# Down projections in blocks of seven products, their sums carried out by ScalarE and accumulating transfers

## The chip, the cores and the metric

The kernel runs on one NeuronCore of a Trainium2 chip. Its engines are TensorE (PE in the profile; PEld is its weight load), VectorE (DVE), ScalarE (ACT), GpSimd (POOL) and SyncE (SP); each works off its own instructions in order and waits on semaphores. Matmuls write into PSUM, which has eight banks of 128 x 512 float32. The metric is device time in microseconds, from the first to the last work of an execution; lower is better.

## The reference, cut to what matters

A two-layer model over 512 tokens with 1024 features. Each layer mixes tokens (spatial gating in the first, attention in the second, both with attention over 256 memory rows) and then has a feed forward with 2816 hidden features:

```python
f = rmsnorm(h, ln_ffn_pre[layer])
f = (jax.nn.silu(f @ w_ffn_gate[layer]) * (f @ w_ffn_up[layer])) @ w_ffn_down[layer]
h = h + rmsnorm(f, ln_ffn_post[layer])
```

All data are float32. The change concerns the last product, `@ w_ffn_down`: (512 x 2816) by (2816 x 1024).

## The kernel before, in words

**Three products for one.** A float32 operand is cut by `split` (L239) into a high part (ScalarE's cast to float32r) and a low part (VectorE's source minus high). `mm3` (L191 to L193) makes a product of three matmuls: high by high, high by low, low by high. So each weight block costs a cast on ScalarE and a subtraction on VectorE before TensorE can use it. Parts of weights stand in eight pairs of slots (tags `hi` and `lo`), raw weights as loaded from memory in four slots of 512 KB (tag `raw`); a split waits for a free pair of slots, a load for a free raw slot. All loads are issued by SyncE.

**The feed forward** (`feed_forward`, L1113) takes the 22 tiles of 128 hidden features in groups. Tiles 0 and 1 are computed at the boundary with the layer's mixing part and their down projection starts the sums `ys[tb][dh]` (four blocks of 128 tokens by two halves of 512 outputs, in SBUF). Then come the groups (2, 8), (8, 14), (14, 18) and (18, 22). For each pair of tiles in a group a `Seven` (L1018) computes gate, and another up: seven products in place of eight over two by two blocks (a Strassen scheme), each product four `mm3` of 256 columns. Its weight sums run on VectorE (`sums`, L1037), its results go to `s1` and `s2` (tag `p`, six slots of 128 x 512) partly by ScalarE's copies out of PSUM (L1059 to L1074) and partly by VectorE's additions (`end`, L1079 to L1082). `gate_rows` (L1132) multiplies by the norm and applies silu, `up_rows` (L1138) multiplies gate and up and splits the product into `fs`, the stationary operand of the down projection. In a `Seven` TensorE uses the PSUM banks of tag `mm` (gate) or `lg` (up), three each; two more have the tag `tr`.

**The down projection of a group** (L1191 to L1200) follows its Sevens: for each half `dh` of the outputs, four PSUM banks, one for each block of tokens; for each pair of hidden tiles a load (`down_weights`), two splits, and 2 x 4 `mm3` of 512 columns; at the end four additions on VectorE (L1200) of a bank onto `ys`. The last group, (18, 22), goes to `tail_of`, which completes the sums and the norm.

**Order.** The kernel is written as a program of tile operations; the framework orders each engine's instructions ahead of time by the order of the program and by a simulated readiness, and adds the semaphores. A tile that is allocated where all slots of its tag are taken waits for the release of one. `behind` adds an order by hand; here it keeps the weight sums of a group's first Seven behind the end of the Seven before.

Of the kernel before, what the change touches and what calls it, by code (L numbers as in the profile page):

```python
# [15 lines left out]
P = 128  # L16
# [3 lines left out]
TB = T // P  # L20
# [13 lines left out]
HALVES = ((0, 256), (256, 512))  # L34
# [6 lines left out]
def hybrid(ctx: ExitStack, tc: tile.TileContext, i: dict, out: bass.AP):  # L41
    nc = tc.nc
# [3 lines left out]
    tp = ctx.enter_context(tc.tile_pool(name="temps", bufs=4))  # L46
    wp = ctx.enter_context(tc.tile_pool(name="weights", bufs=4))
# [17 lines left out]
    def prob(s, shape=(P, T)):  # L65
        return tp.tile(list(shape), F32, tag="p", name=name(s), bufs=6)

    def temp(s, shape=(P, T), tag="t", bufs=4, dt=F32):
        return tp.tile(list(shape), dt, tag=tag, name=name(s), bufs=bufs)

    def small(s, n=4, dt=F32):
        return sp.tile([P, n], dt, tag=f"s{n}", name=name(s))

    def ps(tag, shape=(P, T), s="ps"):
        return pp.tile(list(shape), F32, tag=tag, name=name(s), bufs=2 if tag == "tr" else 3)

    V, A, PE, G = nc.vector, nc.scalar, nc.tensor, nc.gpsimd
# [53 lines left out]
    def pair_of_parts(n=512, aside=False):  # L131
        if aside:
            return act("whi"), act("wlo")
        return (wp.tile([P, max(n, 512)], F32R, tag="hi", name=name("whi"), bufs=8)[:, :n],
                wp.tile([P, max(n, 512)], F32R, tag="lo", name=name("wlo"), bufs=8)[:, :n])

    def cut(pair, w):

        return [(pair[0][:, d : d + w], pair[1][:, d : d + w]) for d in range(0, pair[0].shape[1], w)]
# [24 lines left out]
    def moving_pair(src, aside=False):  # L164

        raw = wp.tile([P, 1024], F32, tag="raw", name=name("raw"), bufs=4)
        last_load[0] = nc.sync.dma_start(raw.rearrange("p (m c) -> p m c", m=4), src)
        four = raw.rearrange("p (m k c) -> p m k c", m=4, k=2)
        parts = []
        for x in range(2):  # L170
            hi, lo = (t.rearrange("p (m c) -> p m c", m=4) for t in pair_of_parts(aside=aside))
            split(four[:, :, x, :], hi, lo)
            parts.append((hi, lo))
        return parts
# [5 lines left out]
    def down_weights(layer, k, dh, aside=False):  # L180
        return moving_pair(i["w_down"][layer, 4 * dh : 4 * dh + 4, :, k : k + 2, :]
                           .rearrange("m p k c -> p m (k c)"), aside)

    def token_products(o, x, w, tb, start, stop):

        c = slice(tb * P, (tb + 1) * P)
        return mm3(o.rearrange("p (m c) -> p m c", c=P), (x[0][:, c], x[1][:, c]), w, start, stop)

    def mm3(o, w, x, start, stop, more=False):

        PE.matmul(o, w[0], x[0], start=start, stop=False, skip_group_check=more)  # L191
        PE.matmul(o, w[0], x[1], start=False, stop=False, skip_group_check=more)  # L192
        return PE.matmul(o, w[1], x[0], start=False, stop=stop, skip_group_check=more)  # L193
# [44 lines left out]
    def split(src, hi, lo, eng=None):  # L238
        last_parts[:] = A.copy(hi, src), (eng or V).tensor_sub(lo, src, hi)  # L239
# [22 lines left out]
    class Norm:  # L262


        def __init__(self, width=T):
            self.r4 = small("r4")
            self.acc, self.width = None, width
# [66 lines left out]
    def parts(s):  # L334
        return [(act(f"{s}hi"), act(f"{s}lo")) for _ in range(KT)]
# [682 lines left out]
    class Seven:  # L1018
# [29 lines left out]
        def product(self, o, w, n, more=False):  # L1048
            for k, w in enumerate(cut(w, P)):
                mm3(o, w, self.xs[n][k], k == 0 and not more, k == KT // 2 - 1, more)  # L1050
# [62 lines left out]
    def feed_forward(layer, phase, xp, meanwhile=None):  # L1113

        nnorm = PairNorm()
        rb = rbc
        groups = ((2, 8), (8, 14), (14, 18), (18, 22))

        def hidden(gate, up, f, cols):
            c0, c1 = cols  # L1120
            n = c1 - c0
            gr = temp("gr")
            V.tensor_mul(gr[:, :n], gate, rb[:, c0:c1])
            s = temp("silu")
            A.activation(s[:, :n], gr[:, :n], AF.Silu)
            ff = temp("f")
            V.tensor_mul(ff[:, :n], up, s[:, :n])
            split(ff[:, :n], f[0][:, c0:c1], f[1][:, c0:c1])

        gates = [None] * 3  # L1130

        def gate_rows(row, g):  # L1132

            V.tensor_mul(g, g, rb)
            gates[2] = A.activation(g, g, AF.Silu, scale=-1.0 if row else 1.0)
            gates[row] = g

        def up_rows(row, u, fs):  # L1138
            if row:
                V.scalar_tensor_tensor(out=u, in0=u, scalar=-1.0, in1=gates[1], op0=ALU.mult, op1=ALU.mult)  # L1140
            else:
                V.tensor_mul(u, u, gates[0])
            split(u, *fs[len(fs) - 2 + row])

        fs = [(act("fhi"), act("flo")) for _ in range(2)]

        def first(n, aside):
            return prepared(i["w_up" if n % 2 else "w_gate"][layer, n // 2], (KT, P), aside)

        def evac_first(outs, cols):  # L1150
            for m in range(2):
                hidden(outs[2 * m], outs[2 * m + 1], fs[m], cols)

        scaled = {}
        a, close = boundary(phase, G_MIX_POST + layer, G_FFN_PRE + layer, nnorm, rb, first, evac_first, scaled)
        w = [down_weights(layer, 0, dh) for dh in range(2)]
        close()
        xs, last = combined(a, scaled, xp)
        last()
        ys = [[plain("y") for _ in range(2)] for _ in range(TB)]  # L1160
        for tb in range(TB):
            for dh in range(2):
                o = ps("lg" if dh else "mm", s="y")
                for k in range(2):
                    token_products(o, fs[k], w[dh][k], tb, k == 0, k == 1)
                A.copy(ys[tb][dh], o)

        for gi, (k0, k1) in enumerate(groups):
            fs = []
            for m in range(k0, k1, 2):  # L1170
                if meanwhile and m == k1 - 2 and gi == len(groups) - 1:
                    next(meanwhile)
                fs += [(act("fhi"), act("flo")) for _ in range(2)]
                sevens((lambda: Seven(xs, lambda n: i["w_gate"][layer, m + n], "mm", gate_rows),
                        lambda: Seven(xs, lambda n: i["w_up"][layer, m + n], "lg",
                                      lambda row, t: up_rows(row, t, fs))), m == 2, m == k0)
            nk = k1 - k0
            if gi == len(groups) - 1:
                if layer:
                    with behind([gates[2]]):  # L1180
                        A.preload_act_table_set("natural_log_exp_and_others")
                if meanwhile:
                    next(meanwhile)

                eps = small("eps")
                V.tensor_mul(eps, nnorm.r4, nnorm.r4)
                V.reciprocal(eps, eps)
                V.tensor_scalar_mul(eps, eps, RMS_EPS)
                return tail_of(fs, lambda kp, dh, aside, k0=k0: down_weights(layer, k0 + 2 * kp, dh, aside), ys, eps,
                               layer == 1)  # L1190
            for dh in range(2):  # L1191
                outs = [ps("mm" if tb < 2 else "lg", s="y") for tb in range(TB)]
                for kp in range(nk // 2):
                    w = down_weights(layer, k0 + 2 * kp, dh)
                    for x in range(2):
                        k = 2 * kp + x
                        for tb in range(TB):
                            token_products(outs[tb], fs[k], w[x], tb, k == 0, k == nk - 1)
                for tb in range(TB):
                    V.tensor_add(ys[tb][dh], outs[tb], ys[tb][dh])  # L1200


    def layer_b(phase, fp):
# [198 lines left out]
    with tc.tile_pool(name="ffn1", bufs=4) as xp:  # L1402
        tail, ys = feed_forward(1, phase, xp)
# [97 lines left out]
```

## Time and profile before

| | |
|---|---|
| time, median of 3 runs (lowest to highest) | 1104.77 us (1104.55 to 1104.82) |
| span of the profiled execution, first to last instruction | 1102.4 us |
| TensorE busy | 1094.9 us (99%) |
| VectorE busy | 887.8 us (81%) |
| ScalarE busy | 679.7 us (62%) |
| GpSimd busy | 23.9 us (2%) |
| loads from HBM | 105.23 MB |

The runs' time is 2.4 us above the span: what lies before the first and behind the last instruction. The profile has no time of its own for the profiled execution beside its span. In the profile "busy" of an engine is time in which at least one of its instructions runs; a matmul's row tells from when to when it was in TensorE's pipeline, and the next starts before its end, so the distance between starts is its price. A row of a view of stages (`A:B`) gives, for a stretch of the run, each engine's busy time with its count of instructions, then the granted TensorE clock, the share of the transfer engines and their GB/s. A row of the timeline gives start, duration, engine, line and operation, and in brackets how long the engine had been idle and what ended that.

### The profile page before, as it was taken

What the parts mean: (1) busy time and instruction counts of PE and PEld (TensorE: products, weight loads), DVE (VectorE), ACT (ScalarE), POOL (GpSimd) and SP (SyncE); (2) the same over time, 40 slices, a digit from 0 to 9 for tenths busy, and PEclk for the clock granted to TensorE, in tenths of its full rate; (3) what the DMA queues carried; (4) which work ended last, traced back from release to release, by engine and by line L of the source; (5) the groups of instructions that cost most, each with busy time, mean ns of one, the idle gap of its engine ahead of it and who ended that gap; (6) DMA issues with size and microseconds to landing.
All of it is one profiled execution on the core that took longest, in us unless ns stands there. A gap on an engine that the chain in (4) does not pass through costs nothing.

```text
span 1102.4 us, 19497 instructions
## 1 busy us (share of the span) xinstructions
PE 1094.9 (99%) x7362; PEld 1001.0 (91%) x7363; DVE 887.8 (81%) x1750; ACT 679.7 (62%) x1428; POOL 23.9 (2%) x40
## 2 busy tenths in 40 slices
PE   9999999999999999999999999999999999999998
PEld 8998889999899899998988998889999899899996
DVE  7879759997698488797968789868997698588776
ACT  7776578664365254477747788868665266255454
POOL 0000000000000000001000000000000000000000
PEclk9999999999999999999999999999999999999999
DMA  7521331334135133245222654531235134233232
GB/s 271 160 78 58 115 115 39 116 115 138 54 115 148 53 106 115 77 153 175 73 80 61 154 130 125 148 115 40 78 97 153 58 114 132 62 114 117 77 97 77
DMA packets 64021, 118.65 MB, mean 108 GB/s; under 512 B 5236, under 2 KB 40072, under 8 KB 63928
## 3 DMA queue, kind: packets, MB, share of 16 engines
q1 hardware_dynamic: 63032, 116.57, 34.7%
q8 instruction: 58, 0.95, 0.4%
q0 software_dynamic: 192, 0.52, 0.2%
q10 hardware_dynamic: 704, 0.32, 0.1%
q14 instruction: 35, 0.29, 0.1%
HBM read 105.23 MB, written 2.10 MB: 97 GB/s over the span
## 4 chain that ended last, share of the span: by engine, by line
PE 95%; DVE 2%; ACT 2%; DMA 0%; issue 0%; SPq 0%; DVEq 0%; ACTq 0%
PE y L191 10%; PE y L192 10%; PE y L193 10%; PE a L191 5%; PE a L193 5%; PE a L192 5%; PE ps L191 4%; PE ps L193 4%; PE ps L192 4%; PE e L191 3%; PE e L193 3%; PE e L192 3%; PE x L193 3%; PE x L191 3%; PE x L192 3%; PE v L191 2%
## 5 line engine op out<-in xcount | busy, mean ns | idle before, releaser
L239 ACT CAST whi<-raw 128x512 fp32r<-128x512 f32 x460 | 277.6, 620 | 260.3 <-PE y L193 118.5
L239 DVE TENSOR_TENSOR wlo<-raw,whi 128x512 fp32r<-128x512 f32 x460 | 306.3, 686 | 116.8 <-ACT whi L239 114.7
L191 PE MATMUL y<-whi,fhi 128*128 128x512 f32 (+1 forms) x356 | 139.6, 393 | 0.0
L193 PE MATMUL y<-whi,flo 128*128 128x512 f32 (+1 forms) x356 | 139.4, 391 | 0.0
L192 PE MATMUL y<-wlo,fhi 128*128 128x512 f32 (+1 forms) x356 | 139.2, 391 | 0.0
L193 PE MATMUL x<-xshi,wlo 128*128 128x256 f32 x320 | 89.8, 281 | 0.0
L191 PE MATMUL x<-xshi,whi 128*128 128x256 f32 x320 | 89.7, 280 | 0.0
L191 PE MATMUL a<-xshi,whi 128*128 128x256 f32 x320 | 89.7, 281 | 0.0
L192 PE MATMUL a<-xslo,whi 128*128 128x256 f32 x320 | 89.7, 280 | 0.0
L192 PE MATMUL x<-xslo,whi 128*128 128x256 f32 x320 | 89.7, 280 | 0.0
L193 PE MATMUL a<-xshi,wlo 128*128 128x256 f32 x320 | 89.6, 281 | 0.0
L193 PEld LDWEIGHTS y<-whi,flo 128*128 128x128 f32 x356 | 66.9, 188 | 15.6 <-DVE flo L239 0.2
L192 PEld LDWEIGHTS y<-wlo,fhi 128*128 128x128 f32 x356 | 66.9, 188 | 14.9 <-DVE wlo L239 0.2
L191 PEld LDWEIGHTS y<-whi,fhi 128*128 128x128 f32 x356 | 66.9, 188 | 14.7 <-ACT fhi L239 0.2
L191 PE MATMUL ps<-xshi,whi 128*128 128x256 f32 (+1 forms) x224 | 68.4, 305 | 0.0
L192 PE MATMUL ps<-xslo,whi 128*128 128x256 f32 (+1 forms) x224 | 66.7, 298 | 0.0
L193 PE MATMUL ps<-xshi,wlo 128*128 128x256 f32 (+1 forms) x224 | 66.3, 298 | 0.0
L191 PEld LDWEIGHTS a<-xshi,whi 128*128 128x128 f32 x320 | 60.3, 188 | 0.3
L192 PEld LDWEIGHTS a<-xslo,whi 128*128 128x128 f32 x320 | 60.2, 188 | 0.4
L191 PEld LDWEIGHTS x<-xshi,whi 128*128 128x128 f32 x320 | 60.2, 188 | 0.0
L193 PEld LDWEIGHTS x<-xshi,wlo 128*128 128x128 f32 x320 | 60.2, 188 | 0.0
L193 PEld LDWEIGHTS a<-xshi,wlo 128*128 128x128 f32 x320 | 60.2, 188 | 0.0
(303 smaller groups left out, 3075.1 us busy)
## 6 DMA issues: line engine op xcount, KB each, us to landing
raw<-in_w_gate SPq DMA_DIRECT2D x44, 512.0 KB, 3.6
raw<-in_w_up SPq DMA_DIRECT2D x44, 512.0 KB, 3.6
raw<-in_w_down SPq DMA_DIRECT2D x44, 512.0 KB, 4.0
raw<-in_w_out SPq DMA_DIRECT2D x16, 512.0 KB, 4.0
raw<-in_w_b_q SPq DMA_DIRECT2D x8, 512.0 KB, 4.3
raw<-in_w_a_v SPq DMA_DIRECT2D x6, 512.0 KB, 8.1
raw<-in_w_a_u SPq DMA_DIRECT2D x6, 512.0 KB
raw<-in_w_v SPq DMA_DIRECT2D x6, 512.0 KB, 3.5
```

Source lines behind the costliest of these rows:

```text
L191: PE.matmul(o, w[0], x[0], start=start, stop=False, skip_group_check=more)
L192: PE.matmul(o, w[0], x[1], start=False, stop=False, skip_group_check=more)
L193: return PE.matmul(o, w[1], x[0], start=False, stop=stop, skip_group_check=more)
L239: last_parts[:] = A.copy(hi, src), (eng or V).tensor_sub(lo, src, hi)
```

## The change

The three middle groups become four of two pairs each: (2, 6), (6, 10), (10, 14), (14, 18); (18, 22) stays as it was. The down projection of a middle group is done by `down_sevens`: for each of its two pairs of tiles, seven products in place of eight over two by two blocks (two hidden tiles by two halves of the tokens on the one side, two hidden tiles by two halves of the outputs on the other). Each product is two `mm3` of 512 columns (for 128 tokens each). `Inner` makes the token side from the two results of the up Seven, in place of the split in `up_rows`; for a group's first pair the low parts of two tiles are made without VectorE: ScalarE writes the negated high part and a transfer adds the source onto it (`split_aside`). `DownSeven` makes the weight side: four sums and seven splits. Products of both pairs that belong to the same sum go on in the same PSUM bank. The results leave PSUM by ScalarE's copies into a tile `yo` of tag `p` and are added to `ys` by accumulating transfers issued from GpSimd (`put`); two banks are carried on by a copy from PSUM to PSUM.

```diff
-        groups = ((2, 8), (8, 14), (14, 18), (18, 22))
+        groups = ((2, 6), (6, 10), (10, 14), (14, 18), (18, 22))
...
-        def up_rows(row, u, fs):
+        def up_rows(row, u, fs, done):
...
-            split(u, *fs[len(fs) - 2 + row])
+            if done:
+                done(row, u)
+            else:
+                split(u, *fs[len(fs) - 2 + row])
+
+        def split_aside(src, hi, lo, aside):
+            if not aside:
+                return split(src, hi, lo)
+            A.copy(hi, src)
+            A.activation(lo, hi, AF.Copy, scale=-1.0)
+            G.dma_start(lo, src, accum_op=ALU.add)
+
+        class Inner:
...
+            def combine(self, u0, u1):
+                left, right = (slice(*c) for c in HALVES)
+                first = tp.tile([P, 2, 256], F32R, tag="acc", name=name("b11"), bufs=2)
+                split(u0[:, left], first[:, 0, :], first[:, 1, :])
+                second, both, other = [(act("fhi"), act("flo")) for _ in range(3)]
+                split(u1, *second)
+                V.tensor_sub(u0[:, left], u0[:, right], u0[:, left])
+                V.tensor_sub(u0[:, right], u1[:, right], u0[:, right])
+                V.tensor_sub(u1[:, right], u0[:, left], u1[:, right])
+                V.tensor_add(u1[:, left], u1[:, right], u1[:, left])
+                split_aside(u0, *both, self.aside)
+                split_aside(u1, *other, self.aside)
+                half = lambda pair, c: tuple(t[:, c] for t in pair)
+                self.x = {1: (first[:, 0, :], first[:, 1, :]), 2: half(second, left), 3: half(second, right),
+                          4: half(other, left), 5: half(both, left), 6: half(other, right), 7: half(both, right)}
+
+        class DownSeven:
+            def __init__(self, pair):
+                self.x = pair.x
+                raws = []
+                for dh in range(2):
+                    raw = wp.tile([P, 1024], F32, tag="raw", name=name("raw"), bufs=4)
+                    last_load[0] = nc.sync.dma_start(
...
+                a11, a12, a21, a22 = (r[:, :, x, :] for r in raws for x in range(2))
+                self.w = {4: a22}
+                s3 = temp("s3").rearrange("p (m c) -> p m c", m=4)
+                V.tensor_sub(s3, a11, a21)
+                self.w[1] = self.parts(a11)
+                V.tensor_add(a21, a21, a22)
+                self.w[2] = self.parts(a12)
+                V.tensor_sub(a11, a11, a21)
+                V.tensor_add(a12, a11, a12)
+                self.w.update({3: a12, 5: a21, 6: a11, 7: s3})
...
+            def product(self, outs, n, start, stop):
+                w = self.w[n]
+                if n > 2:
+                    w = self.parts(w)
+                for x, o in enumerate(outs):
+                    c = slice(x * P, (x + 1) * P)
+                    mm3(o, tuple(t[:, c] for t in self.x[n]), w, start, stop, True)
+
+        def down_sevens(pairs):
+            def put(x, *where):
+                some = prob("yo")
+                A.copy(some, x)
+                for tb, dh in where:
+                    G.dma_start(ys[tb][dh], some, accum_op=ALU.add)
...
+            a, b = DownSeven(pairs[0]), None
+            chain = [ps("tr", s="yc") for _ in range(2)]
+            a.product(chain, 1, True, False)
+            lows = [ps("mm", s="yl") for _ in range(2)]
+            a.product(lows, 2, True, False)
+            shared = [ps(t, s="ys") for t in ("mm", "lg")]
+            a.product(shared, 7, True, False)
+            ups = [ps(t, s="yu") for t in ("lg", "lg")]
+            a.product(ups, 3, True, False)
+            b = DownSeven(pairs[1])
+            b.product(chain, 1, False, True)
+            for x in range(2):
+                put(chain[x], (x, 0))
+            b.product(shared, 7, False, True)
+            for x in range(2):
+                put(shared[x], (x, 1), (x + 2, 1))
+            for u in (a, b):
+                u.product(chain, 6, False, u is b)
+            for x in range(2):
+                A.copy(shared[x], chain[x])
+            b.product(ups, 3, False, True)
+            for x in range(2):
+                final(ups[x], x + 2, 0)
+            a.product(chain, 5, False, False)
+            a.product(shared, 4, False, False)
+            b.product(lows, 2, False, True)
+            for x in range(2):
+                final(lows[x], x, 0)
+            b.product(chain, 5, False, True)
+            for x in range(2):
+                put(chain[x], (x + 2, 0), (x + 2, 1))
+            b.product(shared, 4, False, True)
+            for x in range(2):
+                final(shared[x], x, 1)
...
-            for dh in range(2):
-                outs = [ps("mm" if tb < 2 else "lg", s="y") for tb in range(TB)]
-                for kp in range(nk // 2):
-                    w = down_weights(layer, k0 + 2 * kp, dh)
-                    for x in range(2):
-                        k = 2 * kp + x
-                        for tb in range(TB):
-                            token_products(outs[tb], fs[k], w[x], tb, k == 0, k == nk - 1)
-                for tb in range(TB):
-                    V.tensor_add(ys[tb][dh], outs[tb], ys[tb][dh])
+            down_sevens(pairs)
```

`final(x, tb, dh)` is `put(x, (tb, dh))`.

More of the change, by code (lines that the diff above doesn't have):

```diff
@@ L1142, in up_rows, with __init__, __call__ @@
                 V.tensor_mul(u, u, gates[0])
-            split(u, *fs[len(fs) - 2 + row])
+            if done:
[9 more added lines that the diff above has]
+        class Inner:
+            def __init__(self, k, aside):
+                self.k, self.aside, self.u = k, aside, {}
+            def __call__(self, row, u):
+                self.u[row] = u
+                if len(self.u) == 2:
+                    self.combine(self.u[0], self.u[1])
+            def combine(self, u0, u1):
[13 more added lines that the diff above has]
+                          4: half(other, left), 5: half(both, left), 6: half(other, right), 7: half(both, right)}
@@ new lines, in feed_forward, with parts @@
+        class DownSeven:
[5 more added lines that the diff above has]
+                    last_load[0] = nc.sync.dma_start(
+                        raw.rearrange("p (m c) -> p m c", m=4),
+                        i["w_down"][layer, 4 * dh : 4 * dh + 4, :, pair.k : pair.k + 2, :].rearrange("m p k c -> p m (k c)"))
+                    raws.append(raw.rearrange("p (m k c) -> p m k c", m=4, k=2))
+                a11, a12, a21, a22 = (r[:, :, x, :] for r in raws for x in range(2))
[8 more added lines that the diff above has]
+                self.w.update({3: a12, 5: a21, 6: a11, 7: s3})
+            def parts(self, src):
+                pair = pair_of_parts()
+                split(src, *(t.rearrange("p (m c) -> p m c", m=4) for t in pair))
+                return pair
+            def product(self, outs, n, start, stop):
[5 more added lines that the diff above has]
+                    mm3(o, tuple(t[:, c] for t in self.x[n]), w, start, stop, True)
@@ new lines, in down_sevens, with final @@
+        def down_sevens(pairs):
[4 more added lines that the diff above has]
+                    G.dma_start(ys[tb][dh], some, accum_op=ALU.add)
+            def final(x, tb, dh):
+                put(x, (tb, dh))
+            a, b = DownSeven(pairs[0]), None
[32 more added lines that the diff above has]
+                final(shared[x], x, 1)
@@ L1168, in feed_forward @@
         for gi, (k0, k1) in enumerate(groups):
-            fs = []
+            fs, pairs = [], []
             for m in range(k0, k1, 2):
@@ L1172, in feed_forward @@
                     next(meanwhile)
-                fs += [(act("fhi"), act("flo")) for _ in range(2)]
+                if gi < len(groups) - 1:
+                    pairs.append(Inner(m, m < k1 - 2))
+                else:
+                    fs += [(act("fhi"), act("flo")) for _ in range(2)]
                 sevens((lambda: Seven(xs, lambda n: i["w_gate"][layer, m + n], "mm", gate_rows),
                         lambda: Seven(xs, lambda n: i["w_up"][layer, m + n], "lg",
-                                      lambda row, t: up_rows(row, t, fs))), m == 2, m == k0)
+                                      lambda row, t: up_rows(row, t, fs, pairs and pairs[-1]))), m == 2, m == k0)
             nk = k1 - k0
```

## The prediction

> **What bounds the kernel now.** I read the profile page first: busy times, then the chain of work that ended last.
>
> ```profile
> span 1102.4 us, 19497 instructions
> PE 1094.9 (99%) x7362; PEld 1001.0 (91%) x7363; DVE 887.8 (81%) x1750; ACT 679.7 (62%) x1428; POOL 23.9 (2%) x40
> PE 95%; DVE 2%; ACT 2%; DMA 0%; issue 0%; SPq 0%; DVEq 0%; ACTq 0%
> PE y L191 10%; PE y L192 10%; PE y L193 10%; PE a L191 5%; PE a L193 5%; PE a L192 5%; PE ps L191 4%; PE ps L193 4%; PE ps L192 4%; PE e L191 3%; PE e L193 3%; PE e L192 3%; PE x L193 3%; PE x L191 3%; PE x L192 3%; PE v L191 2%
> ```
>
> 95% of the chain is TensorE, and 30% of it is the y products, to which the down projections belong. A matmul taken away there shortens the run, as long as VectorE and ScalarE still feed TensorE in time. So next the stages of layer 0's feed forward, one row each (Sevens of three pairs, down; three pairs, down; two pairs, down; two pairs):
>
> ```profile
> core 0: us, PE busy (x) PEld busy (x) DVE busy (x) ACT busy (x) POOL busy (x), PEclk, DMA share, GB/s
> 201.60:261.30 59.70, 59.70 (x506) 59.70 (x505) 55.59 (x98) 39.55 (x81) 0.00 (x0) 1.00 0.40 124
> 261.30:294.60 33.30, 33.30 (x145) 26.98 (x145) 18.71 (x31) 8.77 (x15) 0.00 (x0) 1.00 0.27 81
> 294.60:354.40 59.80, 59.80 (x506) 59.76 (x505) 54.09 (x93) 37.13 (x75) 0.00 (x0) 1.00 0.38 115
> 354.40:387.70 33.30, 33.30 (x146) 26.95 (x145) 18.67 (x31) 8.76 (x15) 0.00 (x0) 1.00 0.26 79
> 387.70:427.60 39.90, 39.90 (x339) 39.85 (x338) 34.42 (x59) 24.38 (x49) 0.00 (x0) 1.00 0.39 120
> 427.60:449.90 22.30, 22.30 (x99) 18.00 (x98) 15.89 (x27) 6.28 (x11) 0.00 (x0) 1.00 0.22 72
> 449.90:490.00 40.10, 40.10 (x340) 40.10 (x339) 36.12 (x65) 26.54 (x57) 0.00 (x0) 1.00 0.32 100
> ```
>
> TensorE never pauses here. VectorE is busy 86 to 93% of a Seven stage and 56 to 71% of a down stage. The change takes TensorE work from the stages in which VectorE has air, and gives VectorE more; the question is whether that air is enough. Two views give VectorE's real price and how it meets TensorE at a stage's end: one TensorE row (the first down product after the Sevens) and VectorE's rows behind it.
>
> ```profile
> 427.57 0.40 PE L191 MATMUL y<-whi,fhi 128*128 128x512 f32 x1
> 428.92 0.42 DVE L1080 TENSOR_TENSOR s<-a,s 128x256 f32<-128x256 f32 x1
> 429.25 0.68 DVE L1082 TENSOR_TENSOR s<-x,s 128x512 f32<-128x512 f32 x1
> 429.85 0.68 DVE L1140 SCALAR_TENSOR_TENSOR s<-s,s 128x512 f32<-128x512 f32 x1
> 430.45 0.68 DVE L1142 TENSOR_TENSOR s<-s,s 128x512 f32<-128x512 f32 x1
> 431.05 0.68 DVE L1041 TENSOR_TENSOR s<-raw,raw 128x512 f32<-128x512 f32 x1
> 432.34 0.69 DVE L239 TENSOR_TENSOR wlo<-raw,whi 128x512 fp32r<-128x512 f32 x1
> ```
>
> An instruction of 0.68 us is followed by the next after 0.60, one of 0.42 after 0.33: the ends overlap, so I price VectorE at 0.60 for 512 columns and 0.33 for 256.
>
> ScalarE and the loads run well ahead:
>
> ```profile
> 406.48 11.54 SPq L167 DMA_DIRECT2D raw<-in_w_down  x4
> 430.56 0.62 ACT L239 CAST whi<-raw 128x512 fp32r<-128x512 f32 x1 [2.01 <-PE y L193]
> 431.08 1.14 ACT L239 CAST fhi<-s 128x512 fp32r<-128x512 f32 x2
> ACT whi L239 <- PE y L193: 122.9, 61, 2.2
> ```
>
> The down weights are issued between 406.5 and 418.0, 9.5 us or more before their first use at 427.6. And the cast at 430.56 had waited 2 us for a y product: it waited for a free weight slot, not for data (61 such waits, 122.9 us). So the splits stand up to eight pairs of slots ahead of TensorE; that reserve must absorb any burst.
>
> **The change, part by part.** *Fewer products.* Now a pair of inner tiles takes 2 tiles x 2 output halves x 4 token blocks x 3 = 48 matmuls of 512 columns, afterwards 7 products x 2 halves x 3 = 42. Eight pairs in each of two layers: 96 matmuls fewer.
>
> ```profile
> 427.60:449.90 22.30, 22.30 (x96) 1.00 0.22 72
> ```
>
> This row is the y tile alone on TensorE: 96 matmuls in 22.30 us, 0.232 each. The saving is 96 x 0.232 = 22.3 us. The number and bytes of weight loads stay (two of 512 KB for a pair), so SP's queue issues as many as before.
>
> *VectorE's sum for a pair.* Two Sevens take 8 weight sums, 14 low parts, 2 long end sums, 4 row products and 2 low parts of f at 0.60, and 4 short end sums at 0.33: 19.3 us, against 39.9 / 2 = 19.95 of TensorE. Now the down adds 4 low parts and its share of the y sums. Afterwards the 2 low parts of f go (-1.2); Inner adds one short low part, one long one and four short combinations (0.33 + 0.60 + 1.32 = 2.25), and for a group's second pair two more low parts (1.2); DownSeven adds 4 sums and 7 low parts (6.6); the y sums go. Mean of the two pairs: 19.3 - 1.2 + 2.85 + 6.6 = 27.6 us. TensorE's time is 19.95 + 42 x 0.232 = 29.7. VectorE stands at 93%: it doesn't become the bound, and on average this costs nothing, covered by TensorE. Before it was 24 us of 31 in a group of two pairs, so the cover is nearly used up.
>
> *ScalarE.* It gets, for a group, 6 more weight casts, 10 casts and negations of Inner against 4 before, 12 copies out of PSUM and 2 from PSUM to PSUM.
>
> ```profile
> L1166 ACT COPY y<-y 128x512 f32<-128x512 f32 x16 | 9.4, 587 | 8.2 <-PE y L193 8.1
> ```
>
> At 0.52 us for a cast (two took 1.14, ends overlapped) and 0.59 for a copy, a group of 59.4 us costs ScalarE about 40 us. It is no bound; its order is (third rival).
>
> *Accumulating transfers.* A group has 16 for the sums and 2 for split_aside, each 256 KB, all issued by POOL. The trace of before has no accumulate. POOL's other work, the powers of the norms, comes at the boundaries, a group of Sevens (40 us) behind the last block. The nearest rows for the transfers are POOL's four copies of 128 KB over 64 partitions, and the loads:
>
> ```profile
> 498.05 2.27 POOL L390 DMA_DIRECT2D memk<-memk  x4 [311.99 <-DVE memk L388]
> memk<-memk POOLq DMA_DIRECT2D x4, 128.0 KB, 3.7
> raw<-in_w_gate SPq DMA_DIRECT2D x44, 512.0 KB, 3.6
> q1 hardware_dynamic: 63032, 116.57, 34.7%
> ```
>
> Issue: 0.57 us for 64 rows, so 1.1 for 128, and 1.7 if the second read counts as a third set of rows: 20 to 31 us of POOL in 59.4. Data: q1 moved 116.57 MB in 34.7% of 1102.4 us, 0.305 MB/us; 256 KB take 0.86 us as a copy and up to 1.7 if read twice, 15 to 31 us a group, beside 12 loads of 1.7 (21 us). I take the upper values; still it fits, and nothing waits for a landing soon: split_aside's parts are used a Seven pair (20 us) later, two additions to one y tile are four products (5.6 us) or more apart, against 3.7 to land. Cost zero in the sum; zero to large in the range (second rival). The Trainium skill ("Collectives: The Full Stack", the section on the bandwidth ceiling) says an add in the transfer path costs two source reads where a copy needs one, and so halves the rate; by it the data time is the 1.7 just taken, and the sum stays. No run so far shows it.
>
> *The hand-over from Sevens to down.* Here is a new chain. Its last row product starts at 430.45, 2.9 us after TensorE's end at 427.57, and frees at 431.05. Then the second pair must be combined before its products: half a low part 0.33, a long one 0.60, four combinations 1.32, and `both` behind ScalarE's cast, 0.60 + 0.5: x for b's product 7 stands at 3.5 + 3.35 = 6.85 us. TensorE has five products ahead of it (a's 1, 2, 7, 3, b's 1), 5 x 6 x 0.232 = 6.96. The margin is nil, and the rows at 431.05 and 432.34 show that VectorE's order puts weight work of 0.60 between. I take one such instruction: 0.6 us at each of 8 hand-overs, 4.8. Bounds: 0 when none stands between, 2.4 each (19) with four.
>
> *First group of a layer.* Its Seven stage is VectorE's fullest (55.59 of 59.70 for three pairs), it begins behind the boundary with little reserve, and the first pair's Inner adds 2.25 - 1.2 = 1.05, the second's 3.45 in one burst: 4.5 us in all against a reserve of a few products of 1.42 (19.95 / 14). I take one product late, 1.4 us in each layer, 2.8; bounds 0 and 9.
>
> *Sum.* -22.3 + 4.8 + 2.8 = -14.7. The profiled execution's span is 1102.4; with the 2.4 us around it, it stands at the median 1104.8. 1104.8 - 14.7 = 1090.1 us.
>
> **Rivals.** *1. The reserve swallows every burst:* the whole 22.3 us come, 1082.5. For it: eight slots of reserve and no TensorE pause in any row above, at 93% of VectorE. Against: margin nil at the hand-over.
>
> *2. Slower: the accumulating transfers become the bound.* Place: POOL's queue, in order; twelve copies out of PSUM share six slots with the next Sevens' sums, so a late landing holds ScalarE's next copy, with every cast queued behind it, and then TensorE. It decides from 59.4 / 18 = 3.3 us for each transfer when they go one after another. At the 3.7 us of the landing row, one by one, a group lasts 66.6 us against 39.9 + 22.3 = 62.2 before: 8 x 4.4 = 35 us slower, 1140. Against: the four copies were issued 0.57 us apart, not 3.7, so they don't go one by one. The Trainium skill ("DMA: Bandwidth & Descriptors", anatomy of one DMA) gives 2.0 us plus bytes over 436 GB/s, an estimate of 2.6 us here; by it even the strict series stays below 3.3.
>
> *3. PSUM reuse.* `chain` is read by ScalarE and then accumulated on again, twice in a block, `shared` is written from it, and each has one product (1.39 us) of cover for two copies of 0.59. If ScalarE is late by a whole product at two places in a group, 8 x 2 x 1.39 = 22 us: the gain is gone, 1105. For it: ScalarE has some 15 us of work in a down of 19.5. Against: it runs ahead, as its slot waits show.
>
> *4. VectorE is the bound after all:* at the reported 0.69 (row 432.34) for each instruction a pair takes 27.6 x 0.69 / 0.60 = 31.7 against 29.7, 16 x 2.0 = 32 us, 1115. Against: the starts 0.60 apart.
>
> **How the numbers follow.** The forecast has 0.45, rival 1 0.25, rival 2 0.12, rival 3 0.13, rival 4 0.05. The forecast's own range is 1082 to 1100. The range over the cases, 1081 to 1106, leaves out rivals 2 and 4 and a little of the others. Within 0.2% (2.2 us), which a measurement of this kernel can't tell from no change, lies only the middle of rival 3: 0.05. Faster: 0.45 + 0.25 and half of rival 3, 0.77. Slower: rivals 2 and 4 and a little of rival 3, 0.18.
>
> **What would show it.** In the changed kernel 84 y-like matmuls in a down of two pairs at 0.232 apart, 19.5 us; VectorE at or above 90% over the groups; TensorE gaps only near b's product 7, ended by VectorE or ScalarE, largest in each layer's first group. Rival 2 would show as ScalarE copies to yo or s that waited for a DMA; rival 3 as TensorE waiting for a ScalarE copy of chain; rival 1 as no gaps. A landing time of an accumulate above 6 us, or gaps of a microsecond inside the Seven stages, would make the prediction wrong.

## The result, and the profile after

The changed kernel takes 1174.05 us (median of 4 runs, 1170.39 to 1177.46) against 1104.8: 1.0629 times as long (95% interval 1.0604 to 1.0654). The forecast was 1090.1, the range 1081 to 1106, and the sign was wrong too.

These single lines of the profile page of after answer to those shown of before: busy times, the transfer queue that GpSimd issues to (q0: packets, MB, and their time as a share of the sixteen transfer engines' span), the chain of work that ended last, and the issues with their median time to landing.

```profile
span 1175.5 us, 20095 instructions
PE 1113.2 (95%) x7267; PEld 1009.9 (86%) x7267; DVE 948.6 (81%) x1894; ACT 780.1 (66%) x1636; POOL 149.6 (13%) x184
q0 software_dynamic: 20928, 38.28, 18.4%
PE 66%; DMA 14%; DVE 11%; ACT 4%; issue 3%; POOL 2%; DVEq 0%; SPq 0%; ACTq 0%; POOLq 0%
DMA y<-yo 8%; PE y L191 4%; PE y L192 4%; PE y L193 4%; DVE wlo L239 4%; PE ps L191 4%; DMA raw<-in_w_gate 4%; PE ps L193 4%; PE ps L192 4%; PE a L191 3%; PE a L192 3%; PE a L193 3%; PE e L191 2%; PE x L191 2%; PE e L192 2%
y<-yo POOLq DMA_DIRECT2D x128, 256.0 KB, 9.5
```

TensorE has 95 matmul records fewer (96 by the code), as the change says, but it is idle for 62.3 us of the span instead of 7.5, and the chain, 95% TensorE before, now runs for 14% through transfers, above all the accumulating ones (y<-yo) and the gate's weight loads. Where does it wait? The same stage rows as before, for layer 0: Sevens, block, and so on (columns: stretch and its length, busy time of each engine with its count, granted clock, DMA share, GB/s).

```profile
201.90:241.50 39.60, 39.60 (x337) 39.60 (x336) 36.95 (x68) 26.12 (x55) 1.92 (x2) 1.00 0.43 120
241.50:261.80 20.30, 19.72 (x86) 15.38 (x86) 15.72 (x29) 14.20 (x28) 7.83 (x9) 1.00 0.52 127
261.80:314.50 52.70, 44.30 (x339) 43.55 (x338) 42.14 (x75) 30.62 (x63) 7.87 (x9) 0.90 0.70 161
314.50:334.40 19.90, 19.89 (x86) 15.39 (x84) 17.20 (x32) 13.09 (x25) 7.01 (x8) 1.00 0.60 150
334.40:383.60 49.20, 43.72 (x339) 42.84 (x338) 37.84 (x68) 29.73 (x61) 8.75 (x10) 0.93 0.72 164
383.60:404.70 21.10, 20.29 (x86) 15.28 (x85) 18.90 (x35) 13.98 (x27) 7.01 (x8) 1.00 0.56 140
404.70:454.60 49.90, 43.44 (x338) 42.69 (x337) 38.80 (x69) 29.84 (x61) 8.75 (x10) 0.93 0.70 163
```

The blocks that were changed take 19.9 to 21.1 us, against 22.3 before. The loss lies in the Seven stages behind them, whose products the change does not touch: 49.2 to 52.7 us where the one with no block ahead of it takes 39.6. Each of the three has two long pauses of TensorE, and so has the one behind the fourth block. The timeline of TensorE in the first of them, then ScalarE's and VectorE's rows of the same stretch and the issue of a load on SP (last bracket: idle time before, and what ended it):

```profile
265.61 0.28 PE L193 MATMUL e<-t3hi,wlo 128*128 128x256 f32 x1
268.56 0.39 PE L191 MATMUL x<-xshi,whi 128*128 128x256 f32 x1 [2.67 <-ACT yo L1221]
...
282.91 0.28 PE L193 MATMUL a<-d2hi,wlo 128*128 128x256 f32 x1
288.25 0.58 PE L191 MATMUL e<-t,whi 128*128 128x256 f32 x1 [5.06 <-ACT s L1074]
```

```profile
266.62 0.58 ACT L1221 COPY yo<-yc 128x512 f32<-128x512 f32 x1 [2.17 <-DMA y<-yo]
267.92 0.58 ACT L1221 COPY yo<-ys 128x512 f32<-128x512 f32 x1 [0.71 <-DMA y<-yo]
...
286.64 1.29 ACT L1135 ACTIVATE s<-s 128x512 f32<-128x512 f32 x2 [2.77 <-DVE s L1134]
287.84 0.35 ACT L1074 COPY s<-e 128x256 f32<-128x256 f32 x1
```

```profile
282.45 0.69 DVE L1041 TENSOR_TENSOR s<-raw,raw 128x512 f32<-128x512 f32 x1 [5.23 <-DMA raw<-in_w_gate]
285.93 1.28 DVE L1134 TENSOR_TENSOR s<-s,rbc 128x512 f32<-128x512 f32 x2
```

```profile
271.04 1.74 SPq L144 DMA_DIRECT2D raw<-in_w_gate  x2
```

Two chains, both from the transfers. In the first, the block's last copies out of PSUM (to `yo`) wait for older transfers to land, because their slots of tag `p` are still being read; TensorE's product x needs the PSUM bank that such a copy frees, and stands 2.67 us. In the second, a load of gate weights, issued at 271.04, is there only at 282.4; VectorE stands 5.23 us, its row products come late (285.93), ScalarE's silu behind them (286.64), in ScalarE's order the copy of e at 287.84, and TensorE stands 5.06 us. Over the kernel's eight stages the pauses of the first kind come to 22.9 us and those of the second to 26.4. GpSimd's queue waits too: a transfer onto a y tile on which an earlier one is still adding is not issued before that one has landed, and what stands behind it is held as well. From the list of waits (us in all, times, longest):

```profile
POOL y L1223 <- DMA y<-yo: 17.8, 4, 5.8
```

What this adds to the pauses was not measured by itself. The transfer engines from 249 to 290 us (41 us; a digit of the first row is the busy share, in tenths, of a slice of 1.025 us):

```profile
DMA  0029999999999999999999999999999995167300
q0 software_dynamic: 2304, 4.20, 59.0%
q1 hardware_dynamic: 1152, 4.19, 28.8%
```

By the time of their packets, one block's 16 accumulating transfers (4.20 MB) take the sixteen engines 0.59 x 41 = 24.2 us, 1.5 each, and eight weight loads another 11.8. That is 36 us of packet time, without a break from 252 to 283, though the block is over at 261.8. It fits into these 31 us because packets overlap: the DMA shares in the three rows on the first pause, further down, are above 1. In before the same 41 us hold as many bytes of loads and hardly anything else:

```profile
q1 hardware_dynamic: 2688, 4.19, 33.9%
```

A pause costs a second time. Three short stretches around the first one; the last three figures are the granted clock, the DMA share and the GB/s:

```profile
262.00:269.10 7.10, 3.76 (x29) 3.35 (x28) 4.34 (x8) 3.32 (x7) 1.63 (x3) 1.00 1.11 244
269.10:272.40 3.30, 3.30 (x17) 3.21 (x16) 2.92 (x5) 3.04 (x7) 3.30 (x6) 0.50 1.12 204
272.40:282.90 10.50, 10.50 (x90) 10.50 (x90) 5.27 (x10) 5.03 (x11) 1.23 (x2) 1.00 1.08 252
```

Half a microsecond after TensorE resumes, its clock stands at half for 3.3 us, and matmuls of 256 columns start 0.21 us apart instead of 0.12. Over the kernel the mean granted clock is 0.969: 0.031 x 1175.5 = 36 us, against 1 us before (0.999). So the 73.1 us of span are made up, roughly: idle TensorE +54.8, half clock +35, fewer matmuls -22.3, and 5 or more left over, since a part of the half clock lies in the pauses themselves and is counted twice.

### The profile page after: what moved, and what is told of

It reads as the page before. It is cut to its first block, busy times and chain, and to the rows that moved or that the text cites. A ratio compares the mean times of both kernels' runs of the same rounds, so it can differ in the third digit from the quotient of the medians.

```text
span 1175.5 us, 20095 instructions
## 1 busy us (share of the span) xinstructions
PE 1113.2 (95%) x7267; PEld 1009.9 (86%) x7267; DVE 948.6 (81%) x1894; ACT 780.1 (66%) x1636; POOL 149.6 (13%) x184
## 3 DMA queue, kind: packets, MB, share of 16 engines
q0 software_dynamic: 20928, 38.28, 18.4%
## 4 chain that ended last, share of the span: by engine, by line
PE 66%; DMA 14%; DVE 11%; ACT 4%; issue 3%; POOL 2%; DVEq 0%; SPq 0%; ACTq 0%; POOLq 0%
DMA y<-yo 8%; PE y L191 4%; PE y L192 4%; PE y L193 4%; DVE wlo L239 4%; PE ps L191 4%; DMA raw<-in_w_gate 4%; PE ps L193 4%; PE ps L192 4%; PE a L191 3%; PE a L192 3%; PE a L193 3%; PE e L191 2%; PE x L191 2%; PE e L192 2%
## 5 line engine op out<-in xcount | busy, mean ns | idle before, releaser
L239 ACT CAST whi<-raw 128x512 fp32r<-128x512 f32 x492 | 293.7, 620 | 149.5 <-PE a L192 28.0
L239 DVE TENSOR_TENSOR wlo<-raw,whi 128x512 fp32r<-128x512 f32 x492 | 323.7, 684 | 62.7 <-ACT whi L239 62.0
L1223 POOL DMA_DIRECT2D y<-yo x128 | 111.7, 1325 | 208.2 <-ACT yo L1221 171.3
L191 PE MATMUL x<-xshi,whi 128*128 128x256 f32 x320 | 97.2, 304 | 22.9 <-ACT yo L1221 22.9
L1041 DVE TENSOR_TENSOR s<-raw,raw 128x512 f32<-128x512 f32 x40 | 27.6, 689 | 68.6 <-DMA raw<-in_w_gate 59.7
L191 PE MATMUL e<-t,whi 128*128 128x256 f32 x160 | 50.3, 314 | 26.4 <-ACT s L1074 26.4
L193 PEld LDWEIGHTS x<-xshi,wlo 128*128 128x128 f32 x320 | 67.1, 210 | 0.0
L192 PEld LDWEIGHTS x<-xslo,whi 128*128 128x128 f32 x320 | 66.9, 209 | 0.0
L239 ACT CAST whi<-s 128x512 fp32r<-128x512 f32 x56 | 34.8, 622 | 36.6 <-DVE s L1041 21.0
L191 PEld LDWEIGHTS e<-t,whi 128*128 128x128 f32 x160 | 34.1, 213 | 28.0 <-ACT s L1074 28.0
```

The source lines that it names most:

```text
L1041: V.tensor_add(self.s3, a11, a21)
L1223: G.dma_start(ys[tb][dh], some, accum_op=ALU.add)
```

## The experiments

Ratios are to the kernel before, with 95% intervals. All edits but `e7_regrouped`'s are made to the changed kernel.

**Without the sums.** `e1_no_sums`:

```diff
                 some = prob("yo")
                 A.copy(some, x)
-                for tb, dh in where:
-                    G.dma_start(ys[tb][dh], some, accum_op=ALU.add)
```

> The changed kernel with the 16 accumulating transfers of a block left out: ScalarE's copies into yo stay, ys gets nothing from the middle groups. Theory (the transfers cost it all: 1.3 us of all transfer engines each alone, 2.5 beside loads, in one burst; late landings hold the six slots of yo and s, so ScalarE's copies, the PSUM banks and the raw slots): everything but the transfers stays, so the whole loss goes and the 22.3 us of matmuls show: 1083 to 1092. Rival A (VectorE at 93% and the hand-overs are what costs): 1150 or more, TensorE still pauses at the second gate product. Rival B (PSUM banks read by ScalarE and used again): 1105 to 1130.

1089.61 us, ratio 0.9858 (0.9838 to 0.9878). Lines of its page, then the longest pause of layer 0, which lies in the first group, and the wait behind it in the list of waits:

```profile
span 1087.7 us, 19791 instructions
PE 1078.1 (99%) x7267; PEld 981.5 (90%) x7267; DVE 945.9 (87%) x1894; ACT 776.8 (71%) x1636; POOL 37.8 (3%) x56
q0 software_dynamic: 2496, 4.72, 2.6%
```

```profile
251.34 0.73 PE L191 MATMUL ys<-whi,fhi 128*128 128x512 f32 x2 [1.03 <-ACT fhi L239]
```

```profile
PE ys L191 <- ACT fhi L239: 1.9, 2, 1.0
```

Everything in the prediction but these transfers thus comes to 1089.6, where 1090.1 was forecast; the transfers onto `ys`, with all that waits for them, cost 1174.05 - 1089.61 = 84.4 us.

**Regrouping alone.** `e7_regrouped`, on the kernel before:

```diff
-        groups = ((2, 8), (8, 14), (14, 18), (18, 22))
+        groups = ((2, 6), (6, 10), (10, 14), (14, 18), (18, 22))
```

> The kernel before with the groups of the changed one, (2, 6), (6, 10), (10, 14), (14, 18), (18, 22), and the old down projection. Theory: two hand-overs and 16 additions of VectorE (0.60 each) more in all, hidden behind TensorE: 1104.8 within 0.2%. Rival A (hand-overs between Sevens and down cost by themselves): 1 to 3 us for each of the two more, 1107 to 1111.

1105.17 us, 1.0007 (0.9997 to 1.0017): one hand-over more in each layer costs nothing that can be told from zero.

**More slots.** `e3_ten_slots` puts four of a block's twelve copies into another tag, so that they share no slot with the Sevens' sums:

```diff
+        turns = [0]
+
+        def room():
+            turns[0] += 1
+            n = (turns[0] - 1) % 12
+            if n < 6 or n > 9:
+                return prob("yo")
+            return plain("yo")
...
-                some = prob("yo")
+                some = room()
```

> The changed kernel, with four of a block's twelve copies (the second of lows, chain's last two are among them) put into free slots of the tag y, so that copies out of PSUM and the Sevens' s wait less for landings; the same transfers. Theory, first part (slots are what hands the late landing on to ScalarE and PSUM): the pause at gate's second product (2.7 us, with 1.7 for the halved clock after it) goes, 8 x 4 = 32 us, 1140; the second pause, from loads that share the transfer engines, stays or shrinks. Rival D (only the transfers' rate counts, a slot more or less doesn't): 1165 to 1175.

1172.17 us, 1.0602 (1.0574 to 1.063): no gain to speak of. From its list of waits (who waits for whom: us in all, times, longest), with after's rows for the same two, and for x, behind them:

```profile
DVE s L1041 <- DMA raw<-in_w_gate: 70.9, 18, 12.8
PE e L191 <- ACT s L1074: 40.7, 8, 9.3
```

```profile
DVE s L1041 <- DMA raw<-in_w_gate: 59.7, 18, 5.2
PE e L191 <- ACT s L1074: 26.4, 8, 5.1
PE x L191 <- ACT yo L1221: 22.9, 8, 3.7
```

The wait of x for yo is gone from the list (22.9 us in after), and other waits have taken its place: the second chain has grown by 14.3 us, and smaller waits for ScalarE and VectorE make up the rest. The slots are where the lateness shows first; they are not its cause. What is late is the transfer work as a whole, and the weight loads with it.

**Copies in place of additions.** `e5_plain_copies` leaves `accum_op` out, so that a transfer overwrites `ys` with its part instead of adding:

```diff
-                    G.dma_start(ys[tb][dh], some, accum_op=ALU.add)
+                    G.dma_start(ys[tb][dh], some)
```

> The changed kernel with the block's transfers as plain copies onto ys (no addition, so ys holds the last part alone): same number, bytes written, slots and order. Theory (a second read makes an accumulate slow): a plain copy of 256 KB takes 0.86 us of the engines in place of 1.3, so the burst drains in two thirds of the time: landing 5 to 6 us in place of 9.5, 1120 to 1140. Rival E (the number of transfers from GpSimd or its issue of 0.87 us each sets it, not the read): unchanged, 1174.

1137.5 us, 1.0291 (1.027 to 1.0313), and from its page:

```profile
q0 software_dynamic: 12736, 38.28, 10.5%
y<-yo POOLq DMA_DIRECT2D x128, 256.0 KB, 4.9
```

The same 38.28 MB take 10.5% of the engines' span instead of 18.4%, 119 us instead of 216. Less the 28 us that q0 has without these transfers (e1, 2.6% of 1087.7) that is 91 against 188, or 0.71 against 1.47 for one of the 128: by packet time an accumulate takes twice as long as a copy. Copying in place of adding is thus worth 36.6 us of the 84.4. Why a copy is faster is not shown: `ys` need not be read for it, but it also has fewer packets, (12736 - 2496) / 128 = 80 for a transfer in place of 144. And plain copies of these bytes, in this place, still cost 47.9.

**A quarter of the bytes.** `e10_quarter` keeps the number of transfers and their rows, and adds only the first 128 of 512 columns; three quarters of each sum are left out:

```diff
-                    G.dma_start(ys[tb][dh], some, accum_op=ALU.add)
+                    G.dma_start(ys[tb][dh][:, :P], some[:, :P], accum_op=ALU.add)
```

> The changed kernel with each of the 16 transfers of a block cut to its first 128 of 512 columns (three quarters of the sums are left out): same number, same issue, same waits, a quarter of the bytes. Theory (traffic): 0.33 us of the engines each in place of 1.3, the loss of 84 us falls to 10 or 20, 1100 to 1110. Rival E (the number of transfers, GpSimd's issue or the latency of a landing): 1150 or more.

1098.67 us, 0.9946 (0.9926 to 0.9966).

```profile
PE 1080.1 (99%) x7267; PEld 982.0 (90%) x7267; DVE 945.5 (86%) x1894; ACT 777.4 (71%) x1636; POOL 149.5 (14%) x184
q0 software_dynamic: 20928, 13.12, 9.1%
y<-yo POOLq DMA_DIRECT2D x128, 64.0 KB, 5.9
```

GpSimd is as busy issuing as in after (149.5 against 149.6), the packets are as many, and only 9 of the 84 us are left. So neither the issue nor the number of transfers bounds the kernel: their bytes do. The median landing is no measure of the loss: it is 5.9 us here and 4.9 in e5, which costs 39 us more. Most of these 39 us are the second chain again, as TensorE's waits for the copy of e show, in e5 and then in e10:

```profile
PE e L191 <- ACT s L1074: 24.3, 9, 4.2
PE e L191 <- ACT s L1074: 5.2, 7, 1.9
```

That is 19 us; the half clock is 14 more (0.988 of 1134.8 us; e10 has 1.000). Before it VectorE waits 43.5 us for gate loads in e5 and 25.4 in e10. Why e5's transfers delay the loads so much more, at little more packet time (10.5% against 9.1%) but four times the bytes, stays open.

**The sums on VectorE.** `e2_vector_sums` adds straight from PSUM, as the kernel before does:

```diff
-                some = prob("yo")
-                A.copy(some, x)
                 for tb, dh in where:
-                    G.dma_start(ys[tb][dh], some, accum_op=ALU.add)
+                    V.tensor_add(ys[tb][dh], x, ys[tb][dh])
```

> The changed kernel with each sum added by VectorE straight from PSUM, no copy to yo and no transfer. Theory: VectorE gets 16 x 0.60 = 9.6 us more for a group, 64.8 against 59.4 of TensorE, so it is the bound: 8 x 5.4 = 43 us above 1082.5, some 1126, below the changed kernel's 1174. Rival A (VectorE is already what costs): above 1174 by some 77, 1250. Rival C (the pauses come from elsewhere and the sums don't matter): 1174.

1141.78 us, 1.033 (1.0307 to 1.0354); VectorE is busy for 1019.3 us (90%). Sixteen sums in a block are 9.6 us of VectorE at 0.60, where a down projection of the kernel before needed eight (4.8), and VectorE had no such room. The time is 16 us above the 1126 expected; in the waits, TensorE stands 12.5 us for these sums themselves (product x for a bank), and its clock is at 0.994.

**The sums on GpSimd.** `e4_gpsimd_adds`:

```diff
-                    G.dma_start(ys[tb][dh], some, accum_op=ALU.add)
+                    G.tensor_add(ys[tb][dh], some, ys[tb][dh])
```

> The changed kernel with the copies into yo, and each sum added by a GpSimd tensor addition of two SBUF tiles in place of a transfer. Theory (only the traffic on the transfer engines costs): the loads run free, so 1090 to 1100, if GpSimd needs under 3 us an addition (16 in 59 us). Rival F (GpSimd and VectorE share a way to SBUF, so GpSimd's additions hold up VectorE, which has no air): each addition costs VectorE its own length, 16 x 1 us or more for a group, 55 + 16 = 71 against 59.4 of TensorE, 8 x 12 = 93 us above 1090: 1180 or more.

1201.87 us, 1.0884 (1.0864 to 1.0904), the slowest of all, as rival F had it. Its groups view has GpSimd's additions, and the timeline of GpSimd and VectorE shows why:

```profile
L1223 POOL TENSOR_TENSOR y<-yo,y 128x512 f32<-128x512 f32 x128 | 223.8, 1780 | 159.9 <-ACT yo L1221 159.7
```

```profile
255.30 11.63 POOL L1223 TENSOR_TENSOR y<-yo,y 128x512 f32<-128x512 f32 x7 [2.04 <-ACT yo L1221]
```

```profile
254.33 0.68 DVE L239 TENSOR_TENSOR flo<-s,fhi 128x512 fp32r<-128x512 f32 x1
254.93 9.18 DVE L239 TENSOR_TENSOR wlo<-raw,whi 128x512 fp32r<-128x512 f32 x6
```

While GpSimd adds, six of VectorE's low parts take 9.18 us, 1.5 each, instead of 0.60. Over the kernel VectorE is busy 1079.0 us with the 1894 instructions that take 945.9 in e1. The Trainium skill ("SBUF — State Buffer", Who interferes with whom) says that a VectorE instruction with two SBUF inputs contends with a GpSimd instruction that reads SBUF; the trace agrees, at 1.5 against 0.60.

**The late sums on VectorE.** `e6_late_by_vector` leaves the first ten sums of a block to the transfers and gives VectorE the last six (`add` is a VectorE addition straight from PSUM), so that no copy is late at the block's end:

```diff
...
             b.product(chain, 5, False, True)
             for x in range(2):
-                put(chain[x], (x + 2, 0), (x + 2, 1))
+                add(chain[x], (x + 2, 0), (x + 2, 1))
             b.product(shared, 4, False, True)
             for x in range(2):
-                final(shared[x], x, 1)
+                add(shared[x], (x, 1))
```

> The changed kernel with the last six sums of a block (chain's second results to two places each, shared's last) added by VectorE from PSUM, the first ten by transfers as before. Theory: ten transfers drain before the loads of the next pair of Sevens, and PSUM comes free without a landing: most of the 84 us between 1089.6 and 1174 goes; VectorE gets 3.6 us more a group (58.8 of 59.4), so 1100 to 1120. Rival G (any accumulate beside loads costs in proportion): 10/16 of 84 plus 6/16 of 52, 1089.6 + 52 + 20 = 1161.

1175.56 us, 1.0639 (1.0623 to 1.0655): the expectation fell. The timeline of VectorE in the second Seven stage, then the waits:

```profile
340.30 2.57 DVE L1227 TENSOR_TENSOR y<-yc,y 128x512 f32<-128x512 f32 x4 [3.70 <-DMA y<-yo]
```

```profile
PE x L191 <- DVE y L1227: 48.2, 8, 6.8
```

VectorE's sum goes to a y tile on which an earlier transfer is still adding, and waits for its landing; the bank it would free is the one that TensorE wants. The six transfers fewer were paid back in full by a wait that moved from ScalarE to VectorE.

**A block with 14 sums.** The remaining four kernels change the order of the block so that product 3 stays on the chain (14 sums instead of 16), and split the sums so that one y tile gets them from one engine as far as possible. `e8_fourteen_six`: six by VectorE, onto the second half of the tokens, eight by transfers; `e9_fourteen_ten`: ten by VectorE. In these two a part of the sums on product 4's banks is left out, most likely the chain's, which is copied onto banks of their own with no product on them before; which part it is was not measured. `e11_six_eight` and `e12_four_ten` carry product 4 on the banks of `shared` and leave nothing out: six and four by VectorE, eight and ten by transfers.

```diff
-            ups = [ps(t, s="yu") for t in ("lg", "lg")]
-            a.product(ups, 3, True, False)
...
+            b.product(lows, 2, False, True)
+            for x in range(2):
+                put(lows[x], (x, 0))
             b.product(shared, 7, False, True)
             for x in range(2):
-                put(shared[x], (x, 1), (x + 2, 1))
+                put(shared[x], (x, 1))
+                add(shared[x], (x + 2, 1))
...
-            b.product(ups, 3, False, True)
+            for u in (a, b):
+                u.product(chain, 5, False, u is b)
             for x in range(2):
...
+                add(chain[x], (x + 2, 1))
+            for u in (a, b):
+                u.product(shared, 4, False, u is b)
             for x in range(2):
...
+                put(shared[x], (x, 1))
+            for u in (a, b):
+                u.product(chain, 3, False, u is b)
             for x in range(2):
...
+                add(chain[x], (x + 2, 0))
```

(That is e11; e12 has `put` in the last line.)

> A block rearranged to 14 sums: product 3 is the last and goes on top of chain after its second results are taken, so the two sums of ups go; M4 has banks of its own. Six sums, all onto ys of the second token half, by VectorE from PSUM, eight by transfers onto ys of the first half, so that neither waits for the other on one tile. Theory (transfers cost through their traffic beside loads, VectorE has air for six additions: 58.8 of 59.4): eight transfers of 1.3 us and four loads of 1.7 are 17 us in a block of 20, so the loads are on time: 1095 to 1115. Rival G (cost in proportion to the transfers): 1089.6 + 84 x 8/16 = 1132, and more for VectorE.

> The same rearranged block of 14 sums, ten by VectorE and four by transfers. Theory: VectorE 55.2 + 6.0 = 61.2 against 59.4 of TensorE, 8 x 1.8 = 14 us, transfers nearly free: 1104 to 1112. Rival G: 1089.6 + 84 x 4/16 + 14 = 1125.

> The block of 14 sums once more, with M4 on the banks of shared (after its copies) in place of banks of its own; six sums by VectorE, eight by transfers. Theory: traffic and VectorE as in the run of six and eight before, 1105 to 1118; if it ends below 1104.7 the split pays. Rival B (PSUM reuse costs): 1.4 us more in each block, 1125.

> The same with the last two sums by transfers too: four by VectorE (57.6 of 59.4), ten by transfers. Theory: if traffic beside loads is what costs, two more transfers at a block's end, where the next loads are due, cost more than two additions of VectorE: 1115 to 1135. Rival A (VectorE is the tighter one at 58.8): faster than six and eight, 1100 to 1110.

| kernel | sums by VectorE / by transfers | us | ratio (95%) | landing, us |
|---|---|---|---|---|
| e8_fourteen_six | 6 / 8 | 1114.09 | 1.0079 (1.0058 to 1.0101) | 4.7 |
| e9_fourteen_ten | 10 / 4 | 1120.24 | 1.0142 (1.0127 to 1.0157) | 3.3 |
| e11_six_eight | 6 / 8 | 1120.55 | 1.0142 (1.0125 to 1.0159) | 4.2 |
| e12_four_ten | 4 / 10 | 1119.06 | 1.0138 (1.0123 to 1.0153) | 4.6 |

Halving the transfers brings back 54 of the 69 us (e11), but every sum taken off them lands on VectorE: from e8 to e9, four transfers fewer and four sums more are 6 us slower. Only e8 and e12 end inside the range that their theory gave. e9 is 8 us above its range, e11 2.6 above, and e12, which was to be slower than e11 by its theory, can't be told from it. The number of transfers alone does not set the loss: e6 and e12 have ten to a block, but in e6's second block they are issued within 11.5 us and land after 10.2 in the median of the run, in e12's within 19 and after 4.6, and e12 is 56 us faster. The two differ in more than that, in which sums go to VectorE above all, so the spacing is not shown to be the cause by itself. What is left in e11 are small pauses of TensorE, from its waits:

```profile
PE yc L191 <- ACT ys L1253: 8.4, 8, 1.1
PE yc L191 <- ACT b L239: 6.8, 8, 1.3
```

The first is the copy from bank to bank that the next product on the chain must wait for: the prediction's third rival, at 1.1 us a block. No version that adds every sum beats the kernel before; the two that are faster, e1 and e10, leave sums out.

## Why the prediction was wrong, point by point

*Fewer products:* right. 96 matmuls of 0.232 us are gone, and the blocks take 19.9 to 21.1 us where 19.5 was forecast for their products.

*VectorE's sum, ScalarE's, the hand-over, the first group:* right together, by e1: 1082.5 us without any of these costs was rival 1, 1089.6 was measured, so they come to 7.1 us where 4.8 + 2.8 were forecast. That the sum came within half a microsecond is luck in part. The place was right: TensorE's two longest pauses in the feed forwards of e1 are at product 7 in the first group of each layer, ended by ScalarE's cast. But they come to 1.9 us, and the other hand-overs have no pause of 0.6 us at product 7; by e1's timeline the rest is spread over the blocks in gaps of at most 0.6 us. VectorE, forecast at 93% of a group, is busy for 225.4 of the 238.1 us of layer 0's four groups in e1 (95%) and did not become the bound (rival 4); the regrouping is free (e7). Rival 3 came neither there nor in after, where the chain's products wait under a microsecond in all for ScalarE's copies.

*Accumulating transfers, "Cost zero in the sum":* this is the step that failed, by 84.4 us. Its upper value for the data was nearly right: 1.7 us a transfer, 1.5 measured by packet time. What failed is what was done with it:

- It was set against a group ("15 to 31 us a group" in 59.4, "still it fits"). But the transfers come in a block of 20 us and its weight loads stand beside them, also those for the next Sevens. 24.2 us of transfers and 11.8 of loads fill the engines from 252 to 283, and the load that is wanted in that time comes late. An average over the group hides this queue of 31 us.
- "nothing waits for a landing soon" overlooked who does: the next copy into a slot of tag `p`, and the next transfer onto the same y tile. The 3.7 us to land came from four copies of half the bytes with nothing behind them; in the queue it was 9.5 in the median, above the 5.6 us that were to lie between two additions to one tile.
- The prediction's own sign for this, "a landing time of an accumulate above 6 us, or gaps of a microsecond inside the Seven stages", came up at 9.5 us and at gaps of 2.67 and 5.06.

*Rival 2* named the place rightly (twelve copies on six slots, ScalarE held, casts behind it, then TensorE), and its sign is in the waits: ACT yo waits for DMA y<-yo. It was priced too low, at 35 us for transfers one by one at 3.7, and it left out two parts: the weight loads that share the engines, which carry the second pause of each stage (26.4 us against 22.9 for the first) and most of TensorE's waiting once the slots are eased (e3), and the half clock that goes with each pause, some 36 us. Its point of decision was wrong as well: the transfers were not in strict series (1.5 us each, below its 3.3), and it came about all the same.

The two cited rules: two source reads at half the rate (the Trainium skill, "Collectives: The Full Stack", the section on the bandwidth ceiling) agrees with e5 in its size (1.47 us against 0.71), though not alone in its cause, since the packets differ as well. The Trainium skill's formula for one transfer ("DMA: Bandwidth & Descriptors", anatomy of one DMA), from which 2.6 us was estimated, has no queue in it: with four transfers to a block (e9) the median landing is 3.3 us, with sixteen (after) 9.5.

## What to carry to other kernels

Set a burst of transfers against the stretch into which it falls, together with the loads that run there, and not against the mean of a stage; then look for who waits for a landing, slots included. Where TensorE is at 99%, a pause can cost a second time through the clock: in after 62 us of idle time went with up to 36 us of half clock. And before sums are put on a "free" engine or queue, count them: seven products needed 14 to 16 sums a block where eight products needed 8, and with VectorE above 85% neither VectorE, nor GpSimd, nor the transfers could take them for the 15 us that the products save.

## What the runs showed of the hardware

- TensorE's clock went to half in or right behind each of the sixteen pauses of 2.4 to 5.1 us in after's Seven stages, eleven times for 3.4 us and five times for 6.8. The Trainium skill ("TensorE: Matmul & The Clock Gate", Part 1: The HAM clock gate) puts this at one idle window of about 3.4 us or more; here 2.67 us were enough (rows 268.56 and 269.10:272.40), so the measurement decides. The length of a pause alone does not: half clock followed one of 1.77 us in e8 (at 314.13), and none followed one of 2.52 us in e12 (at 469.86).
- A 256 KB transfer that accumulates from SBUF onto SBUF took 1.47 us of the sixteen engines' packet time in a queue of them, a copy 0.71; with a quarter of the bytes in as many packets (e10) it took 0.56 (9.1% of 1095.7, less the same 28, over 128), which is 38%, not 25%. Packets overlap, so the engines get through more than that: at the 204 GB/s of row 269.10:272.40 the 256 KB take 1.3 us.
- An addition of 128x512 with both inputs in SBUF took GpSimd 1.78 us beside a busy VectorE, and VectorE's own then took 1.5 instead of 0.60: in the 9.18 us of the row, six of VectorE's and some five of GpSimd's, where VectorE alone does fifteen.
